# Two chunks of three units by feature tile in the input phase, the third chunk later, and head 1 behind group 0

## The chip, the cores and the metric

The kernel runs on one core of one Trainium2 chip. The metric is device time in microseconds (us) of one execution. A core has a matrix engine (PE, whose weight loads are shown as PEld), three engines for elementwise work (DVE, ACT, POOL) and a queue engine (SP) that issues most transfers. Each engine runs its own list of instructions in the order in which the program wrote them, and waits on semaphores for the others.

## The reference, cut to what matters

One step of a two-layer decoder over 1032 tokens (1024 of a prompt and 8 single samples, T = 1032), with 1024 features and fp32 data. Each layer begins with a modulated norm and one input projection, whose output is cut into four retention heads (v, k, q, g) and four gating groups (vv, u):

```python
mod = jax.nn.silu(c) @ w_ada + b_ada
sh1, sc1, gt1, sh2, sc2, gt2 = jnp.split(mod, 6, axis=-1)
h = modulate(rmsnorm(x, g_mix), sh1, sc1)      # rmsnorm(x)*g * (1 + sc1) + sh1
p = h @ w_in
q, k, v, g, u, vv = jnp.split(p, [...])
...                                             # retention heads, gating groups
mix = jnp.concatenate([o_ret, o_gm], axis=-1) @ w_out
x = x + gt1[:, None, :] * mix
...                                             # norm, up projection, conv, down projection
```

## The kernel before

Features lie on the 128 partitions (8 feature tiles k), tokens on the free axis, cut into three chunks of 344 columns. A **unit** is 128 output features for all 1032 tokens. Each fp32 product is made of three passes of fp32r products, hi*Hh, hi*Hl and lo*Hh, where `hi` and `lo` are the two parts of the weights (`split`: ACT copies hi, DVE subtracts for lo) and `Hh` and `Hl` those of the scaled input. A unit is thus 8 x 3 x 3 = 72 matmuls (L274 in `block`, L261 to L263 in `mm3`). The row factor of the norm (1/rms of each token) is not in Hh: it is multiplied in when the unit leaves PSUM (`rows_out`, L609, by the tile `R`).

PSUM holds two `big` buffers of three banks and two `side` buffers of one bank. The `tp` pool has 23 slots, which weights (`raw`, `hi`, `lo`), modulation weights (`ada`) and activations share.

**Start of layer 0.** All eight tiles of the scale part of `w_ada` are loaded and multiplied (`Ada.part`, L569), then transposed (L578), and only then are Hh (L419) and Hl (L420) made, chunk by chunk. `joint` computes the first two units (v and k of head 0) chunk by chunk. The sums of squares, `rsqrt` and their spread over the partitions (`inv_rms`, `spread`, L393) run beside it, and the shift part of `w_ada` (t0) between chunks 1 and 2. Both units are evacuated at the end. The units q and g of head 0 follow with `unit`.

**Side work.** What follows an evacuation (rotary product, transposes, retention state, group norm) are generators in the list `Side`. `tick` runs at most two steps of them after each feature tile of a unit; `drain` runs them with no unit work between until given tasks are done. The remaining parts of `w_ada` (`ada_t`, parts 2 to 5) are such tasks with the lowest priority.

**Order of units in layer 0, before:** head 0 (v, k, q, g), head 1, group 0, group 1, then the first output projection `partial`, whose three summands are head 0, head 1 and group 0 (`OUT_GROUPS[0] = (0, 1, 4)`). `mixes` drains the last task of these three first. The task chain of a head ends with `task_q` (retention, `row_norm`) and `task_o` (two halves of transposes, product with g, `split`). Nothing else orders the engines.

Of the kernel before, what the change touches and what calls it, by code (L numbers as in the profile page):

```python
# [43 lines left out]
BUDGET = 2  # L44
ADA = (1, 0, 2, 3, 4, 5)
KB = 1.31


class Task:
# [41 lines left out]
def tile_hybrid_decoder_step(  # L91
# [56 lines left out]
    for l in range(DEPTH):  # L148
# [240 lines left out]
    def spread(w, js=range(4)):  # L389

        r = sps()
        for j in js:
            nc.tensor.matmul(  # L393
                r[:, j * QW:(j + 1) * QW], ident[:, 32 * j:32 * j + 1].to_broadcast([128, 128]), w,
                start=True, stop=True)
        return r

    def to_dram(w):
        rd = dp.tile([4, QW], F32, tag="rd", name=f"rd{count[0]}")
        nc.gpsimd.dma_start(out=rd, in_=w[0:128:32])  # L400
        return rd
# [21 lines left out]
    def norm(c, hold, R, A, B, gate=None, dma=True):  # L423
# [6 lines left out]
        if dma:  # L430
            rd = to_dram(w)
        if c == 2 or not dma:
            r = spread(w, (3,) if dma else range(4))
        yield 1
        o = R[:, c * CW:c * CW + n]
        if dma:
            from_dram(o, rd)
        else:
            nc.scalar.activation(out=o, in_=r[:, 0:n], func=ACTF.Copy)
        if c == 2:  # L440
            q = small([128, KT, NB], "gs")
            ss = slice(SEQ, T)
            rb = r[:, CW - NB:CW].unsqueeze(1).to_broadcast([128, KT, NB])
            nc.vector.tensor_tensor(out=q, in0=XS, in1=rb, op=ALU.mult)
            nc.vector.tensor_tensor(out=q, in0=q, in1=A[:, :, 1:9], op=ALU.mult)
            nc.vector.tensor_tensor(out=q, in0=q, in1=B[:, :, 1:9], op=ALU.add)
            nc.scalar.activation(out=Hh[:, :, ss], in_=q, func=ACTF.Copy)
            nc.vector.tensor_tensor(out=Hl[:, :, ss], in0=q, in1=Hhf[:, :, ss], op=ALU.subtract)

    def norm_out(c, hold, xg, g, out, gate=None):  # L450

# [152 lines left out]

    def rows_out(ps, R, name):

        a, b = slot(name), small([128, 1], "wb", 4)
# [328 lines left out]
    with tc.manual_schedule():  # L936
# [9 lines left out]
        nc.vector.memset(ones_m, RS / D)  # L946
        nc.scalar.activation(out=scond, in_=craw, func=ACTF.Silu)

        def load_x(c, ms=slice(0, KT)):
            s = slice(c * CW, (c + 1) * CW)  # L950
            nc.sync.dma_start(out=X[:, ms, s], in_=xT[:, ms, s])

        A, B = mods[0][1], mods[0][0]
        adas[0].issue(8)
        W.issue(1)
        for ms in GROUPS3:
            load_x(0, slice(ms[0], ms[-1] + 1))
        W.issue(2)
        load_x(1)
        load_x(2)  # L960
        adas[0].issue(16)
# [5 lines left out]
        for c in range(NC3):  # L967
            for ms in GROUPS3:
                late = []
                scaled(c, ms, A, late)  # L970
                for f in late:
                    f()
                if c == 0 and ms[0] == 0:
                    W.prepare()
            for ms in GROUPS3:
                squares(c, ms, holds[c])
        next(ns[2])
        next(ns[0])
        t0 = adas[0].part(0, 8)

        def steps(*gs):
            for g, n in gs:
                for _ in range(n):
                    next(g, None)

        def start(c, i):
            if (c, i) == (1, 1):
                steps((t0, 2))
            if (c, i) == (2, 0):
                steps((ns[2], 1), (t0, 4), (ns[2], 1), (t0, 1), (ns[2], 1))  # L990
                columns(B)
                steps((ns[0], 1), (ns[1], 1))
            if (c, i) == (2, 1):
                steps((ns[0], 2), (ns[1], 1))
            if c == NC3:
                steps((ns[1], 2))

        for l in range(DEPTH):
            mod = mods[l]
# [181 lines left out]
```

## Time and profile before

| | us |
|---|---|
| median of three runs | 2087.15 (2087.12 to 2088.16) |
| profiled execution, whole | 2088.26 |
| its span in the trace | 2086.1 |
| PE busy | 2030.7 (97%) |
| DVE, ACT, POOL busy | 1173.6, 663.0, 69.6 |
| first product of a unit starts | 19.12 |
| head 0 (four units) multiplied | 95.34 |
| first product of the first `partial` | 230.32 |

All times are counted from the start of the span. A row of the trace's list of instructions gives the start, the busy time, engine, line, operation, output and inputs, how many instructions it merges, and in brackets how long the engine had been idle before and what ended that. A busy time includes a modelled tail of the matmul, so the spacing of two starts is the better price of one.

### The profile page before, as it was taken

Reading aid. Unit: us, or ns where it says so; the run is one execution under the profiler, and the core shown is the slowest. Engines: PE = TensorE matmul, PEld = TensorE weight load, DVE = VectorE, ACT = ScalarE, POOL = GpSimd, SP = SyncE. Lnnn points to the kernel's source line nnn. Section 1 sums busy time; section 2 is a strip of 40 time slices with the busy share of each in tenths; the row PEclk is TensorE's granted clock in tenths of the full one; section 3 lists DMA queues with packets and bytes.
Section 4 is the critical chain, followed back from the end, with each engine's and each line's share of the span. In section 5 each row is a group of like instructions: output and inputs, shape, how many; then the busy total and the mean of one; then the engine's idle time right before and its main releaser. Section 6 shows DMA issues by size and latency. Waiting matters only on the chain.

```text
span 2086.1 us, 32232 instructions
## 1 busy us (share of the span) xinstructions
PE 2030.7 (97%) x13806; PEld 1970.5 (94%) x13806; DVE 1173.6 (56%) x2087; ACT 663.0 (32%) x903; POOL 69.6 (3%) x155
## 2 busy tenths in 40 slices
PE   7999999999999999999999999999999999999997
PEld 5898999998898999999989999999999999999997
DVE  5356635676544456454673675457846545645566
ACT  4332223224422222324343331332433332241432
POOL 0000000000000000000000000000000000000001
PEclk9999999999999999999999999999999999999998
DMA  9344112112454211111121211121121011111012
GB/s 376 129 145 161 61 51 63 52 59 82 164 195 165 93 51 51 33 59 31 54 68 65 73 56 37 63 73 52 42 58 62 31 51 51 51 41 51 31 34 83
DMA packets 51886, 164.31 MB, mean 79 GB/s; under 512 B 6864, under 2 KB 14384, under 8 KB 51744
## 3 DMA queue, kind: packets, MB, share of 16 engines
q1 hardware_dynamic: 47616, 151.22, 21.6%
q0 software_dynamic: 3728, 10.50, 1.5%
q8 instruction: 109, 1.79, 0.3%
q10 hardware_dynamic: 400, 0.53, 0.1%
q14 instruction: 33, 0.27, 0.0%
HBM read 152.88 MB, written 9.61 MB: 78 GB/s over the span
## 4 chain that ended last, share of the span: by engine, by line
PE 86%; DVE 7%; ACT 3%; DMA 2%; issue 1%; SPq 0%; POOL 0%; POOLq 0%; DVEq 0%; ACTq 0%
PE big L274 74%; PE side L569 2%; DMA ada<-in_w_ada 2%; PE big L261 1%; PE big L262 1%; PE big L263 1%; PE side L618 1%; DVE lo L220 1%; DVE X L516 1%; ACT Hh L419 1%; ACT sq L351 1%; DVE Hl L420 1%; PE side L759 1%; PE side L730 1%; PE side L781 1%
## 5 line engine op out<-in xcount | busy, mean ns | idle before, releaser
L274 PE MATMUL big<-Hh,hi 128*128 128x344 f32 (+1 forms) x2496 | 546.8, 327 | 1.9 <-DVE v L609 1.9
L274 PE MATMUL big<-Hh,lo 128*128 128x344 f32 (+1 forms) x2496 | 533.5, 322 | 7.9 <-DVE lo L220 7.9
L274 PE MATMUL big<-Hl,hi 128*128 128x344 f32 (+1 forms) x2496 | 532.3, 321 | 0.0
L274 PEld LDWEIGHTS big<-Hh,lo 128*128 128x128 f32 x2496 | 423.1, 190 | 9.0 <-DVE lo L220 9.0
L274 PEld LDWEIGHTS big<-Hh,hi 128*128 128x128 f32 x2496 | 415.4, 190 | 17.0 <-issue 14.4
L274 PEld LDWEIGHTS big<-Hl,hi 128*128 128x128 f32 x2496 | 422.6, 189 | 0.0
L609 DVE TENSOR_TENSOR a<-big,R 128x1032 f32<-128x1032 f32 x64 | 78.9, 1233 | 270.6 <-ACT wb L608 270.6
L220 DVE TENSOR_TENSOR lo<-raw,hi 128x1024 fp32r<-128x1024 f32 x160 | 195.0, 1219 | 58.6 <-ACT hi L211 58.6
L899 DVE SCALAR_TENSOR_TENSOR c<-a,pars,c 128x1032 f32<-128x1032 f32 x128 | 165.0, 1290 | 111.4 <-ACT acol L892 77.7
L319 DVE SCALAR_TENSOR_TENSOR X<-big,mod,X 128x1032 f32<-128x1032 f32 x128 | 165.3, 1292 | 108.7 <-PE big L274 108.7
L608 ACT ACTIVATE wb<-big 128x1 f32<-128x1 f32 x112 | 18.9, 169 | 628.8 <-PE big L274 585.4
L211 ACT ACTIVATE hi<-raw 128x1024 fp32r<-128x1024 f32 x160 | 166.7, 1047 | 20.2 <-PE big L274 16.5
L274 PE MATMUL big<-ahi,hi 128*128 128x344 f32 x624 | 132.7, 321 | 0.0
L274 PE MATMUL big<-ahi,lo 128*128 128x344 f32 x624 | 131.8, 319 | 0.0
L274 PE MATMUL big<-alo,hi 128*128 128x344 f32 x624 | 131.7, 319 | 0.0
L274 PEld LDWEIGHTS big<-ahi,hi 128*128 128x128 f32 x624 | 104.2, 188 | 2.9 <-issue 1.6
L274 PEld LDWEIGHTS big<-alo,hi 128*128 128x128 f32 x624 | 104.6, 188 | 0.0
L274 PEld LDWEIGHTS big<-ahi,lo 128*128 128x128 f32 x624 | 104.3, 188 | 0.0
L889 ACT ACTIVATE a<-a,wb 128x1032 f32<-128x1032 f32 x64 | 74.1, 1158 | 83.5 <-DVE a L609 83.5
L925 ACT ACTIVATE ahi<-c 128x1032 fp32r<-128x1032 f32 x32 | 34.2, 1068 | 194.3 <-DVE c L923 192.5
L890 ACT ACTIVATE c<-a,pars 128x1032 f32<-128x1032 f32 x64 | 80.1, 1251 | 3.3
L261 PE MATMUL big<-Hh,hi 128*128 128x344 f32 (+1 forms) x192 | 64.3, 335 | 7.7 <-DVE X L516 5.0
(199 smaller groups left out, 2363.9 us busy)
## 6 DMA issues: line engine op xcount, KB each, us to landing
ada<-in_w_ada SPq DMA_DIRECT2D x96, 512.0 KB, 4.8
raw<-in_w_up SPq DMA_DIRECT2D x64, 512.0 KB, 3.5
raw<-in_w_in SPq DMA_DIRECT2D x48, 512.0 KB, 3.6
raw<-in_w_down SPq DMA_DIRECT2D x32, 512.0 KB, 3.5
raw<-in_w_out SPq DMA_DIRECT2D x16, 512.0 KB, 3.5
S<-in_s_ret POOLq DMA_DIRECT2D x8, 512.0 KB, 4.1
vb<-vd SPq DMA_DIRECT2D x8, 512.0 KB, 4.6
out_rs<-S POOLq DMA_DIRECT2D x8, 512.0 KB, 4.6
```

What stands on the lines that cost most here:

```text
L211: nc.scalar.activation(out=hi[:, 0:1024], in_=self.raw[i][:, 0:1024], func=ACTF.Copy)
L220: nc.vector.tensor_tensor(out=lo[:, 0:1024], in0=self.raw.pop(i)[:, 0:1024], in1=self.split[i][0].bitcast(F32)[:, 0:1024], op=ALU.subtract)
L261: nc.tensor.matmul(out, whi, rhi, start=start, stop=False)
L262: nc.tensor.matmul(out, whi, rlo, start=False, stop=False)
L274: nc.tensor.matmul(ps[:, c, 0:n], w, r[:, s], start=st, stop=sp_)
L319: nc.vector.scalar_tensor_tensor(out=v3(X[:, m]), in0=ps[:, :, 0:CW], scalar=gt[:, m, 0:1], in1=v3(X[:, m]), op0=ALU.mult, op1=ALU.add)
L569: nc.tensor.matmul(ps[32 * j:32 * j + 32, 0:256], scond[:, k, :], w[:, j * 256:(j + 1) * 256], start=(k == 0), stop=(k == KT - 1), tile_po ...
L609: nc.vector.tensor_tensor(out=v3(a), in0=ps[:, :, 0:CW], in1=v3(R), op=ALU.mult)
L889: nc.scalar.activation(out=a[:, 0:T], in_=a[:, 0:T], func=ACTF.Identity, bias=b)
L890: nc.scalar.activation(out=c[:, 0:T], in_=a[:, 0:T], func=ACTF.Identity, scale=w[2], bias=col(l, P_CB + i))
L899: nc.vector.scalar_tensor_tensor(out=c[:, off:off + T], in0=a[:, 0:T], scalar=wt, in1=c[:, off:off + T], op0=ALU.mult, op1=ALU.add)
L925: nc.scalar.activation(out=hi[:, 0:T], in_=c2[:, 0:T], func=ACTF.Copy)
```

## The change

It touches only layer 0 up to the first `partial`.

- The scale part is no longer summed over all features first. `scale_weights(j)` loads for feature tiles 2j, 2j+1 only (two transfers of 512 KB, rows of 1 KB), `scale_sums` multiplies, `scale_out` adds the four partial sums and transposes with the 0/1 matrix `sel`. X is loaded by feature tile (rows of 4128 B), and `operand(m)` makes Hh and Hl of one tile for all 1024 prompt tokens.
- `warm(n)` issues n matmuls of 512 columns on a constant tile `wm`, which nothing reads: 9, 2 and 7 of them before the first real product.
- The first three units (v, k, q) run with the feature tile as the outer loop, over two chunks, in six banks of the two `big` buffers.
- All rows' squares are summed at once (`row_sums`), one `rsqrt` over 258 columns, three `spread`s, and R is ready for the two chunks' evacuation (`first_chunks`).
- `fourth` then runs the remaining shift products, two chunks of unit g, and the third chunk of all four units, and evacuates v, k, q and g one after another.
- In layer 0 group 0 now comes ahead of head 1, in the list of weight pieces and in the order of units: head 0, group 0, head 1, group 1, `partial`.
- `shift = adas[0].part(0, 2)` is the same generator as before, on an `Ada` object on which nothing was issued by then; its `issue` counts tiles from 0.

```diff
-        for p in h0[2:] + head(1) + group(0) + group(1):
+        for p in h0[2:] + (head(1) + group(0) if l else group(0) + head(1)) + group(1):
...
-        adas[0].issue(8)
...
-        side.drain(side.add(adas[0].part(1, 8, 1)))
-        W.prepare()
         R = rows_scale()
-        holds = [[], [], []]
-        ns = [norm(c, holds[c], R, A, B, dma=False) for c in range(NC3)]
...
+        wm = slot("wm", F32R)
+        nc.vector.tensor_copy(wm[:, 0:512], ones_m[:, 0:1].to_broadcast([128, 512]))
+        warm(9)
+        shift = adas[0].part(0, 2)
+        sw = {0: scale_weights(0)}
+        W.issue(1)
+        load_x(0)
...
+        t = scale_sums(sw[0])
+        warm(2)
+        scale_out(0, t)
+        warm(7)
+        W.high()
+        operand(0)
+        W.low()
+        operand(1)
...
+        for j in range(4):
+            order = [(2 * j + kk, i) for kk in range(2) for i in range(3)]
+            if j == 3:
+                order.sort(key=lambda q: q[1])
+            for n, (k, i) in enumerate(order):
+                hi, lo = W.tile(u, i * 8 + k)
+                passes(hi, lo, k, [(place[i][c][0][:, place[i][c][1], 0:CW], c * CW, CW) for c in range(2)])
...
+                if j < 3 and n == SUMS[j]:
+                    t = scale_sums(sw[j + 1])
+                if j < 3 and n == SUMS[j] + 2:
+                    scale_out(j + 1, t)
+                    operand(2 * j + 2)
+                    operand(2 * j + 3)
...
+                if j == 1 and n == 5:
+                    next(shift)
...
+                if j == 3 and n == 0:
+                    w = row_sums()
+                if j == 3 and n == 2:
+                    next(shift)
+                if j == 3 and n == 3:
+                    rows(w, rs8)
+                    first_chunks(0)
+                if j == 3 and n == 5:
+                    first_chunks(1)
+        first_chunks(2)
+
+        def fourth(evac):
+            for _ in range(3):
+                next(shift)
...
+            ps = big()
+            for k in range(KT):
+                hi, lo = W.tile(u4, k)
+                passes(hi, lo, k, [(ps[:, c, 0:CW], c * CW, CW) for c in range(2)])
...
+            rest = big()
+            for i in range(4):
+                out = (rest[:, i] if i < 3 else ps[:, 2])[:, 0:CW + 2]
+                for k in range(KT):
+                    hi, lo = W.tile(u, i * 8 + k) if i < 3 else W.tile(u4, k)
+                    passes(hi, lo, k, [(out, 2 * CW, CW + 2)])
...
-                joint(ev[:2], (), range(NC3), start)
+                fourth(ev)
...
-            run_units(ev[2:])
-            run_units(heads[1].evacs())
-            run_units(grps[0].evacs())
+            run_units(ev[4 if l == 0 else 2:])
+            for o in (heads[1], grps[0]) if l else (grps[0], heads[1]):
+                run_units(o.evacs())
             run_units(grps[1].evacs())
```

**PE at the start of the program, before.** `ada` and `scond` are the modulation's factors, `big` is a unit's accumulator:

```order
L569 MATMUL side_144<-ada_115,scond 32x256 x4
L569 MATMUL side_144<-ada_117,scond 32x256 x4
L578 MATMUL side_179<-ident,adat_177 128x128 x2
L261 MATMUL big_282<-Hh,hi_184 128x344
L262 MATMUL big_282<-Hl,hi_184 128x344
L263 MATMUL big_282<-Hh,lo_188 128x344
```

**PE at the start of the program, now:**

```order
L1014 MATMUL side_107<-wm_105 128x512 x9
L972 MATMUL side_145<-ada_117,scond 32x256 x4
L972 MATMUL side_145<-ada_119,scond 32x256 x4
L1014 MATMUL side_156<-wm_105 128x512 x2
L982 MATMUL side_159<-sel_103,adat_154 128x16 x2
L1014 MATMUL side_164<-wm_105 128x512 x7
L1008 MATMUL big_192<-Hh,hi_172 128x344 x2
L1008 MATMUL big_192<-Hl,hi_172 128x344 x2
L1008 MATMUL big_192<-Hh,lo_176 128x344 x2
```

Two groups of modulation products stand ahead of the first product where eight stood, and 18 constant products stand around them.

**PE at the end of group 1's unit u and the start of the first `partial`, before.** `big_1939` is the unit, `big_2143` the first output tile of `partial`; `hi_1502` and `hi_1993` are weights and a head's mix:

```order
L274 MATMUL big_1939<-Hl,hi_1835 128x344 x2
L274 MATMUL big_1939<-Hl,hi_1835 128x346
L274 MATMUL big_1939<-Hh,lo_1898 128x344 x2
L274 MATMUL big_1939<-Hh,lo_1898 128x346
L274 MATMUL big_2143<-hi_1502,hi_1993 128x344 x3
L274 MATMUL big_2143<-lo_1503,hi_1993 128x344 x3
```

**The same place of PE now.** L568 is a modulation step, L846 and L863 are group 1's transposes and gating products, L619 and L804 the transposes of head 1's output `o` and `os`:

```order
L568 MATMUL side_2025<-ada_2081,scond 32x256 x4
L568 MATMUL side_2025<-ada_2083,scond 32x256 x4
L846 MATMUL side_2114<-ident,os_1898 128x128
L863 MATMUL side_2120<-wst_518,vn_1826 128x128 x4
L568 MATMUL side_2025<-ada_2102,scond 32x256 x4
L568 MATMUL side_2025<-ada_2104,scond 32x256 x4
L619 MATMUL side_2136<-ident,o_1987 128x128 x4
L863 MATMUL side_2142<-wst_518,vn_1826 128x128 x4
L619 MATMUL side_2149<-ident,o_1987 128x128 x4
L804 MATMUL side_2155<-ident,os_1924 128x128
L275 MATMUL big_2165<-hi_1568,hi_1863 128x344 x3
L275 MATMUL big_2165<-lo_1569,hi_1863 128x344 x3
```

Between the unit and `partial` stands side work with no unit's products among it.

**DVE at that place, before.** `u_2120` is the unit's evacuation, `X<-big_2143` takes the first output of `partial`, L632 and L634 belong to group 1's norm:

```order
L188 TENSOR_TENSOR lo_2052<-mix_1923,hi_2051 128x1032
L220 TENSOR_TENSOR lo_2091<-raw_1837,hi_2046 128x1024
L629 BN_STATS st_2097<-vn_1956 128x6 x8
L629 BN_STATS st_2097<-os_2072 128x6
L609 TENSOR_TENSOR u_2120<-big_1939,R_190 128x1032
L632 BN_AGGR mv_2098<-st_2097 128x2 x9
```

**DVE at that place now**, from the last step of head 1's norm (`o_1987`) to the second part of its mix (`lo_2162`):

```order
L645 TENSOR_SCALAR o_1987<-o_1987,mv_2039,fac_2040 128x128 x8
L645 TENSOR_SCALAR os_1924<-os_1924,mv_2039,fac_2040 128x128
L849 TENSOR_SCALAR vrows<-side_2114,pars 128x8
L850 TENSOR_SCALAR ss_2116<-vrows,pars 128x8
L865 SCALAR_TENSOR_TENSOR mix_2119<-side_2120,pars,bsb_519 128x512
L869 TENSOR_TENSOR mix_2119<-mix_2119,u_2010 128x512
L800 SCALAR_TENSOR_TENSOR mix_2127<-side_2136,pars,g_1690 128x512
L865 SCALAR_TENSOR_TENSOR mix_2119<-side_2142,pars,bsb_519 128x512
L869 TENSOR_TENSOR mix_2119<-mix_2119,u_2010 128x512
L800 SCALAR_TENSOR_TENSOR mix_2127<-side_2149,pars,g_1690 128x512
L806 SCALAR_TENSOR_TENSOR mix_2127<-side_2155,pars,g_1690 128x2 x4
L189 TENSOR_TENSOR lo_2162<-mix_2127,hi_2161 128x1032
```

Before, head 1's mix was split on DVE ahead of the last unit's evacuation; now its norm and split come behind it.

## Rows read from the trace of the kernel before

**Rows 1.** Busy time by stretch: length, then PE, PEld, DVE, ACT, POOL; clock, DMA share, GB/s.

```profile
0.00:19.12 19.12, 9.33 (x66) 1.92 (x66) 1.22 (x4) 3.66 (x6) 4.54 (x12) 1.00 0.92 333
19.12:59.34 40.22, 37.15 (x306) 33.38 (x306) 27.55 (x69) 22.39 (x40) 0.64 (x1) 1.00 0.95 365
...
95.34:230.32 134.98, 131.25 (x1010) 119.89 (x1009) 74.31 (x198) 39.60 (x56) 5.24 (x7) 1.00 0.41 139
230.32:2086.10 1855.78, 1821.36 (x12211) 1787.27 (x12209) 1059.75 (x1808) 585.30 (x786) 56.22 (x132) 1.00 0.20 65
```

**Rows 2.** List of instructions, PE at the start, and the last slow products.

```profile
13.15 2.29 PE L569 MATMUL side<-ada,scond 128*32 128x256 f32 x16 [0.19 <-DMA ada<-in_w_ada]
...
17.23 0.69 PE L578 MATMUL side<-ident,adat 128*128 128x128 f32 x2 [0.50 <-ACT adat L574]
...
29.34 0.49 PE L262 MATMUL big<-Hl,hi 128*128 128x344 f32 x1
...
29.62 0.45 PE L263 MATMUL big<-Hh,lo 128*128 128x344 f32 x1
...
29.91 0.33 PE L261 MATMUL big<-Hh,hi 128*128 128x344 f32 x1
```

**Rows 3.** The same list, PE where `joint` ends and the next units begin.

```profile
58.33 1.02 PE L393 MATMUL side<-rw,ident 128*128 128x86 f32 x8
61.29 0.75 PE L274 MATMUL big<-Hh,hi 128*128 128x344 f32 x3 [1.95 <-DVE v L609]
...
64.94 1.23 PE L274 MATMUL big<-Hh,lo 128*128 128x344 f32 x3 [2.42 <-DVE lo L220]
...
71.10 1.07 PE L569 MATMUL side<-ada,scond 128*32 128x256 f32 x16
```

**Rows 4.** The same list, DVE: a weight's lo, a 1032-column product, an rsqrt step.

```profile
18.37 1.22 DVE L220 TENSOR_TENSOR lo<-raw,hi 128x1024 fp32r<-128x1024 f32 x1
...
434.00 1.28 DVE L319 SCALAR_TENSOR_TENSOR X<-big,mod,X 128x1032 f32<-128x1032 f32 x1
...
50.08 0.25 DVE L341 SCALAR_TENSOR_TENSOR rw<-rw 128x86 f32<-128x86 f32 x1
```

**Rows 5.** Transfers, first 60 us: GB/s in 40 slices of 1.5 us; issue to landing.

```profile
GB/s 0 150 306 418 399 394 297 393 407 426 393 372 387 399 371 377 369 377 372 414 418 401 421 399 429 407 423 403 407 397 423 385 415 415 412 145 262 257 183 22
...
ident<-in_ident POOLq DMA_DIRECT2D x1, 64.0 KB, 3.9
```

**Rows 6.** The chain of waits by merged pieces: a long run of unit products.

```profile
249.57 32.70 PE big L274 x207
```

**Rows 7.** List of instructions, an evacuation and a head's norm near the second `partial`.

```profile
402.17 1.23 DVE L609 TENSOR_TENSOR u<-big,R 128x1032 f32<-128x1032 f32 x1 [6.18 <-ACT wb L608]
...
403.44 1.16 ACT L823 ACTIVATE u<-u,wb 128x1032 f32<-128x1032 f32 x1 [1.30 <-DVE u L609]
...
405.06 0.70 DVE L632 BATCH_NORM_AGGREGATE mv<-st 128x2 f32<-128x6 f32 x9
...
407.90 2.13 DVE L644 TENSOR_SCALAR vn<-vn,mv,fac 128x128 f32<-128x128 f32 x8
...
410.21 2.14 DVE L644 TENSOR_SCALAR o<-o,mv,fac 128x128 f32<-128x128 f32 x8
```

**Rows 8.** The same list, head 1's last steps before the first `partial`.

```profile
217.50 1.16 PE L862 MATMUL side<-wst,vn 128*128 128x128 f32 x8 [0.84 <-DVE mix L799]
...
218.69 0.75 DVE L864 SCALAR_TENSOR_TENSOR mix<-side,pars,bsb 128x512 f32<-128x512 f32 x1 [1.25 <-PE side L862]
...
219.48 0.69 DVE L868 TENSOR_TENSOR mix<-mix,u 128x512 f32<-128x512 f32 x1
...
220.23 0.60 DVE L805 SCALAR_TENSOR_TENSOR mix<-side,pars,g 128x2 f32<-128x2 f32 x4
...
220.87 1.06 ACT L187 ACTIVATE hi<-mix 128x1032 fp32r<-128x1032 f32 x1 [7.83 <-DVE mix L805]
...
221.96 1.23 DVE L188 TENSOR_TENSOR lo<-mix,hi 128x1032 fp32r<-128x1032 f32 x1 [1.13 <-ACT hi L187]
```

More of the change, by code (lines that the diff above doesn't have):

```diff
@@ L46 @@
 KB = 1.31
+SUMS = (2, 1, 1)
 class Task:
@@ L429, in norm @@
         yield 5
[L430 to L433, printed above, removed]
+        rd = to_dram(w)
+        if c == 2:
+            r = spread(w, (3,))
         yield 1
[L435 to L439, printed above, removed]
-        if c == 2:
[L441 to L448, printed above, removed]
+        from_dram(R[:, c * CW:c * CW + n], rd)
+        if c == 2:
+            samples(r[:, CW - NB:CW], A, B)
     def norm_out(c, hold, xg, g, out, gate=None):
@@ L605, in rows_out @@
     def rows_out(ps, R, name):
+        if isinstance(ps, tuple):
+            return ps
         a, b = slot(name), small([128, 1], "wb", 4)
@@ L955, in tile_hybrid_decoder_step, with warm @@
+        def warm(n):
+            ps = sps()
+            for _ in range(n):
+                nc.tensor.matmul(ps, wm[:, 0:128], wm[:, 0:512], start=True, stop=True)
+        wm = slot("wm", F32R)
[3 more added lines that the diff above has]
+        sw = {0: scale_weights(0)}
         W.issue(1)
-        for ms in GROUPS3:
-            load_x(0, slice(ms[0], ms[-1] + 1))
-        W.issue(2)
+        load_x(0)
@@ L959, in tile_hybrid_decoder_step @@
         load_x(1)
-        load_x(2)
-        adas[0].issue(16)
-        side.drain(side.add(adas[0].part(1, 8, 1)))
-        W.prepare()
-        R = rows_scale()
-        holds = [[], [], []]
-        ns = [norm(c, holds[c], R, A, B, dma=False) for c in range(NC3)]
[L967 to L996, printed above, removed]
+        W.issue(3)
@@ new lines, in tile_hybrid_decoder_step @@
+        for j in (1, 2):
+            sw[j] = scale_weights(j)
+            load_x(2 * j)
+            load_x(2 * j + 1)
+        load_x(6)
+        load_x(7)
+        R = rows_scale()
+        t = scale_sums(sw[0])
[6 more added lines that the diff above has]
+        operand(1)
+        W.high()
+        W.low()
+        W.high()
+        W.low()
+        u = list(W.get()) + list(W.get())
+        banks = [big(), big()]
+        place = [[(banks[(2 * i + c) // 3], (2 * i + c) % 3) for c in range(2)] for i in range(3)]
@@ new lines, in tile_hybrid_decoder_step, with row_sums @@
+        sums = []
+        def row_sums():
+            q = small([128, KT, NB], "gs")
+            nc.scalar.activation(out=q, in_=XS, func=ACTF.Square)
+            for a, ms in zip(sums, GROUPS3):
+                nc.vector.tensor_reduce(
+                    out=a[:, SEQ:T], in_=q[:, ms[0]:ms[-1] + 1].rearrange("p m b -> p b m"), axis=AX.X, op=ALU.add)
+            ps = sps()
+            for i, a in enumerate(sums):
+                av = a[:, 0:T].rearrange("p (c q n) -> p q c n", c=NC3, q=4)
+                for j in range(4):
+                    nc.tensor.matmul(
+                        ps[32 * j:32 * j + 32, 0:NC3 * QW].rearrange("p (c n) -> p c n", c=NC3), ones_m, av[:, j],
+                        start=(i == 0), stop=(i == 2), tile_position=(0, 32 * j))
+            w = slot("rw")[:, 0:3 * NC3 * QW].rearrange("p (s n) -> p s n", s=3)
+            nc.vector.tensor_scalar(
+                out=w[:, 0], in0=ps[:, 0:NC3 * QW], scalar1=EPS * RS, scalar2=None, op0=ALU.add)
+            rsqrt(w[:, 0], w[:, 1], w[:, 2])
+            return w[:, 1]
@@ new lines, in rows, with square @@
+        def rows(w, rs8):
+            for c in range(NC3):
+                n = CW if c < 2 else CW - NB
+                r = spread(w[:, c * QW:(c + 1) * QW])
+                nc.scalar.activation(out=R[:, c * CW:c * CW + n], in_=r[:, 0:n], func=ACTF.Copy)
+                if c == 2:
+                    nc.scalar.activation(out=rs8, in_=r[:, n:CW], func=ACTF.Copy)
+        def square(m):
+            t = slot("sq")
+            nc.scalar.activation(out=t[:, 0:SEQ], in_=X[:, m, 0:SEQ], func=ACTF.Square)
+            if m in (0, 3, 6):
+                sums.append(t)
+            else:
+                a = sums[-1]
+                nc.vector.tensor_tensor(out=a[:, 0:SEQ], in0=a[:, 0:SEQ], in1=t[:, 0:SEQ], op=ALU.add)
```

101 lines of the change are left out of this document (97 added, 4 removed).

## Prediction

> **What bounds the kernel now.** I read the stretches first, then the list of instructions at the two places that the change rewrites. PE is busy for 131.25 of 134.98 us between the end of head 0's products and the first `partial`, and for 1821 of 1856 us after it [rows 1]. A unit's matmul costs 32.70/207 = 0.158 us there [rows 6], so in both stretches the sum of matmuls is the time, and only PE's gaps can be won or lost. Head 0 is different: its 288 matmuls are 288 x 0.158 = 45.5 us, and they end at 95.34. Three losses are visible. The first product starts at 19.12, behind eight modulation tiles [rows 1, 2]. PE then runs slowly until about 29.9: two starts are 0.28 us apart [rows 2] against 0.158, which is the lower of the two clock levels (1.2 against 2.4 GHz), although the clock column says 1.00. After `joint` PE waits 1.95 us for v's evacuation and 2.42 us for the next weights, and the products that start at 64.94 are slow again (1.23 us for three); by 71.10 a modulation step of 16 records takes 1.07 us instead of 2.29 [rows 2, 3].
>
> The span is 2086.1 us in the profiled execution and the median is 2087.15, so I add 1.05 us to a span.
>
> **Part 1, up to the first dense product (S).** The constant products need `wm`, whose cast stands behind the reduction of `ident` on DVE, and `ident` needs 3.9 us to land after an early POOL issue [rows 5]: about 5.5, and 6.3 with the two DVE steps. Nine products of 512 columns at the slow price (512/344 x 0.285 = 0.43 us) end at 10.2. The two modulation groups behind them cost 2.29 [rows 2]: 12.5. Copying the sums takes about 0.5, the selector 0.5 (between the slow 0.69 of the transposes [rows 2] and half of it), the two small DVE steps 0.5, Hh of tile 0 on ACT 1.05 (as a copy of 1032 columns [rows 8]): 15.1. Then DVE is the engine that PE waits for: Hl, lo, Hl, lo, lo stand in this order, at 1.15 to 1.25 us each [rows 4]: 21.1. With the last products of tile 0, **S = 21.4**. I take the clock as fast by then: before, the products from 19.12 ran slow and those after 29.9 fast [rows 2], and here products begin at 6.3. If the clock is slow at S, because PE waits between 15 and 21, the next products run at half speed, as those from 64.94 to 71 did [rows 3], which costs 2.5 to 3 us more. Ends: S = 19.8 (fast from 10) to 24.
>
> **Part 2, from S to the fourth unit (F).** PE has 126 matmuls (19.9), three sums of modulation (3 x 1.07), three selectors (0.8), row sums (12 matmuls of 258 columns, about as long as 1.5 modulation groups of 256: 1.6), three spreads at 1.0 each [rows 3] and four shift steps at 1.07: 32.8 us. Waits: each new pair of feature tiles needs selector, DVE, ACT and DVE again (0.5 + 1.05 + 1.25), of which 6 or 12 matmuls (1.0 or 1.9 us) hide a part, so PE waits about 1.7, 0.7 and 0.8 us; the row sums wait for the last Hl and its reductions (0.7); nine rsqrt steps over 258 columns (0.25 for 86 [rows 4], so about 0.43 each, 3.9 us) lie under 18 matmuls and a shift step (3.9 us) with 0.3 us left. That is 4.2, and F = 21.4 + 37 = 58.4.
>
> Transfers set a second bound. `shift` counts tiles from 0, so its first `issue` loads eight scale tiles that nothing reads (4.2 MB), ahead of the ten that are used. Up to the last shift tile 21.5 MB are to be moved; at the 400 GB/s of the slices from 4.5 to 52.5 us [rows 5] that ends near 56.5, and its product at 57.6. The two bounds fall together, and I keep F = 58.4. Rows of 1376 B (X, the slices from 16.5 to 28.5) move at about 375 GB/s against some 410 of the 4 KB rows [rows 5]; the new 1 KB rows (4.2 MB) may lose as much and the longer X rows win it back.
>
> The Trainium skill (DMA: Bandwidth & Descriptors, Specifications) gives about 358 GB/s as a core's limit from HBM. By it the fourth unit would start near 64 and the sum below would be 5 to 6 us higher; the slices of the trace stay near 400 for 45 us, so I give that 0.03.
>
> **Part 3, end of head 0.** 48 matmuls and the transposes of the shift are 7.9 us; 96 matmuls of 346 columns and v's transposes 16.1. Head 0 is multiplied at 58.4 + 24.0 = **82.4** instead of 95.34: 12.9 us earlier. The first part of the change works.
>
> **Part 4, what comes behind.** Against the 131.25 us of PE work from there to `partial` [rows 1], 4.0 us are added, because part 2 of `w_ada` (four steps at 1.0), which before ran inside head 0's units, now runs behind; and 1.9 us move from behind the start of `partial` to ahead of it (group 1's transposes and gating products, now drained). The first unit of group 0 needs the `big` buffer of g, which is evacuated last: 2.1 us of waiting, like the 1.95 of v [rows 3]. ACT reloads its function tables twice more; nothing waits for ACT there.
>
> **The drain** is the largest term. Head 1 is now followed by two units instead of four. Its chain does not fit under them: in the new order of PE all of it, from the last output product of head 1 on, stands between group 1's last product and `partial`, with no unit's products among it, and the rest of part 5 of `w_ada`. From the last product (t = 0): evacuation of u starts at 0.4, ACT is done with it at 2.8 [rows 7], copies the second half of o (0.6), DVE takes its statistics (1.0): 4.5. From the aggregation to the end of the scaling of vn and o are 7.3 us [rows 7]: 11.8, and two small steps, 12.4. From here the transposes and gating products go one behind another, since one `side` buffer is held by the modulation sums; the trace shows that wait (0.84 us on DVE's mix) [rows 8]. A gating product with its DVE step takes 217.50 to 219.44, 1.94 us, a half of o's transposes about 1.4 beside the second gating step of 0.69 [rows 8]: 14.3, 15.7, 17.7, 19.1. From the last small DVE products to lo are 220.23 to 223.19, 3.0 us: **22.4**. Queued behind this on PE is the whole `partial`: nine products on head 0's mix can go at 19.4, the rest waits for hi and lo. Useful PE work within the 22.4 us: output products 1.75, four modulation steps at most 4.0, the transposes and gating products 2.4, and 12 products of `partial` 1.9, together 10.1. So PE idles 12.3 us, 7 of them in one piece. Gaps of 1.95 and 2.42 us close together were enough to lose the fast clock before [rows 3]; I add 2.6 us for about 5.5 us of products at half speed, as from 64.94 to 71. Before, this place cost 134.98 - 131.25 = 3.7 us with all gaps of the stretch; 0.9 of them lie earlier and stay.
>
> **Sum.** 82.4 + 131.25 + 4.0 + 1.9 + (2.1 + 0.9 + 12.3 + 2.6) = 237.5 for the start of `partial` at full rate, and 1855.8 - 1.9 behind it: 2091.4, against 2086.1. The time is 2091.4 + 1.05 = **2092**, 0.25% slower. In short: 12.9 us won, 4.0 only moved, 14 lost again in the gaps.
>
> **The rivals.**
> - *The gain is kept (faster).* If the drain costs little, the start's 12.9 less 4.0 and 2.1 remain: 2080 to 2082. It decides at a drain of under 5 us in all (gap and clock). For it: DVE is busy only 74 of 135 us there [rows 1], so steps could start earlier than I chain them. Against it: PE's order is fixed, and head 1's norm alone takes 12 us of DVE and ACT after the last product. 0.11.
> - *The start is lost too (slower).* The clock is slow at S, or the shift tiles land late because SP waits for slots ahead of them. From the point where F lies beyond 62, the time is 2096 to 2100. For it: from 15 to 21 PE waits for DVE between pairs of products. Against it: S moves little, and a gap of 1.95 us followed by products left them fast at 61.29 [rows 3]. 0.14, with the transfer limit above.
> - *A wash.* S and F at their early ends and a short slow spell after the drain: 2087 to 2089, no change to be measured. 0.17.
> - The forecast's case, 2089 to 2096: 0.58.
>
> **How the numbers follow.** A measurement of this kernel can tell about 0.2%, 4.2 us, from no change: the limits are 2083 and 2091.3. The forecast's case lies for six parts in ten above the upper one: 0.36 slower, 0.22 the same. With the rivals, slower 0.50, same 0.39, faster 0.11. The range 2083 to 2099 leaves out most of the first rival and the end of the second.
>
> **What would show it.** Right: the ninth constant product ends near 10, the dense products begin near 21 with 0.158 us spacing, head 0 ends at 80 to 85, and ahead of the first `partial` PE has about 12 us of idle time behind DVE, followed by some 5 us of products 0.28 us apart. Wrong: PE idle for under 6 us there; slow products between 21 and 30; a wait of over 3 us for shift tiles ahead of the fourth unit; or new waits after `partial`, which I take as unchanged.

## The result, and the profile after

The changed kernel takes **2112.35 us** (2111.4 to 2113.97) against 2087.35 (the kernel before, with a fourth run beside the three of its table): a ratio of 1.012 (95% interval 1.0102 to 1.0137), 25 us slower, and beyond the end of the predicted range. The profiled span is 2109.6 us, 18.2 above the sum of 2091.4.

The stretches of core 0 come first; the columns are the stretch, its length, the busy time of each engine with its count of records, PE's granted clock, DMA share and GB/s:

```profile
core 0: us, PE busy (x) PEld busy (x) DVE busy (x) ACT busy (x) POOL busy (x), PEclk, DMA share, GB/s
0.00:21.78 21.78, 13.43 (x56) 9.15 (x57) 8.16 (x11) 9.01 (x10) 4.53 (x12) 0.90 0.95 327
21.78:24.40 2.62, 2.62 (x20) 1.35 (x20) 0.00 (x0) 0.39 (x1) 0.00 (x0) 0.51 1.07 396
24.40:61.98 37.58, 33.80 (x281) 26.98 (x280) 20.84 (x33) 15.45 (x20) 0.00 (x0) 1.00 0.95 374
61.98:88.82 26.84, 24.66 (x160) 24.02 (x156) 4.22 (x11) 10.82 (x17) 1.74 (x3) 1.00 0.22 76
88.82:227.73 138.91, 130.66 (x986) 117.68 (x985) 71.52 (x174) 40.73 (x57) 7.16 (x8) 0.99 0.40 138
227.73:257.00 29.27, 21.57 (x130) 13.80 (x130) 18.23 (x63) 5.36 (x8) 0.00 (x0) 0.65 0.49 176
257.00:2109.60 1852.60, 1817.35 (x12171) 1783.18 (x12169) 1048.33 (x1772) 581.80 (x781) 56.46 (x132) 1.00 0.20 65
```

The marks are: the last product of feature tile 0 ends at 21.78 (the prediction's S), the clock rises at 24.40, the fourth unit starts at 61.98 (F), head 0 is multiplied at 88.82, group 1's last product of a unit ends at 227.73, and `partial` runs at full rate by 257. Before, head 0 ended at 95.34 and `partial` began at 230.32 [rows 1].

PE's own list at the start (start, busy time, engine, line, operation, tiles, records; the wait ahead in brackets) answers to [rows 2]:

```profile
6.28 4.21 PE L1014 MATMUL side<-wm 128*128 128x512 f32 x9 [6.28 <-DVE wm L1017]
10.41 1.19 PE L972 MATMUL side<-ada,scond 128*32 128x256 f32 x16
...
14.40 0.58 PE L1008 MATMUL big<-Hh,hi 128*128 128x344 f32 x2
...
19.19 0.94 PE L1008 MATMUL big<-Hh,lo 128*128 128x344 f32 x2 [0.79 <-DVE lo L221]
...
21.78 1.93 PE L972 MATMUL side<-ada,scond 128*32 128x256 f32 x16
...
24.38 0.49 PE L1008 MATMUL big<-Hl,hi 128*128 128x344 f32 x2
```

Sixteen modulation records take 1.19 us at 10.41, behind the constant products, and 1.93 at 21.78: the clock had risen and fallen again while PE waited between tile 0's products.

The rest of head 0 has these rows, the sums and spreads of the squares and then the third chunks; they answer to [rows 3]:

```profile
46.88 1.95 PE L1060 MATMUL side<-sq,ones_m 128*32 128x258 f32 x24
...
54.61 1.12 PE L394 MATMUL side<-rw,ident 128*128 128x86 f32 x8 [0.55 <-ACT R L1073]
...
74.73 0.42 PE L1008 MATMUL big<-Hh,hi 128*128 128x346 f32 x1 [0.88 <-DVE v L1163]
...
80.55 0.43 PE L1008 MATMUL big<-Hh,hi 128*128 128x346 f32 x1 [1.30 <-DVE k L1163]
```

Between 88.82 and 227.73 PE idles 8.25 us, in seven waits. Three of them, with the DVE rows ahead of the last:

```profile
108.53 0.66 PE L619 MATMUL side<-ident,vv 128*128 128x128 f32 x4 [0.78 <-ACT kt L718]
112.84 0.66 PE L619 MATMUL side<-ident,vv 128*128 128x128 f32 x4 [1.35 <-DVE S L738]
...
179.96 1.23 DVE L189 TENSOR_TENSOR lo<-mix,hi 128x1032 fp32r<-128x1032 f32 x1 [3.33 <-ACT hi L188]
...
183.52 1.23 DVE L665 TENSOR_TENSOR k<-k,ks 128x1032 f32<-128x1032 f32 x1
184.67 0.23 DVE L580 TENSOR_TENSOR mod<-side,pars 128x72 f32<-128x72 f32 x1
184.89 1.09 PE L619 MATMUL side<-ident,k 128*128 128x128 f32 x4 [3.00 <-DVE mod L580]
```

A step of one chain (vv's or k's transposes) stands in PE's order, the row puts its wait down to a step of another chain on ACT or DVE, and the unit's products wait behind it. (For the wait of 3.00 us the step that the row names isn't the one, see e8.) The other four waits are 0.84, 0.52, 0.69 and 1.08 us, the last for a tile of `w_ada` at 207.34. The drain ahead of `partial` is the place of [rows 8]:

```profile
232.11 0.68 PE L568 MATMUL side<-ada,scond 128*32 128x256 f32 x8 [2.43 <-ACT u L824]
...
235.63 1.08 PE L568 MATMUL side<-ada,scond 128*32 128x256 f32 x8 [1.24 <-DMA ada<-in_w_ada]
...
243.33 1.94 PE L568 MATMUL side<-ada,scond 128*32 128x256 f32 x16
...
247.16 1.16 PE L863 MATMUL side<-wst,vn 128*128 128x128 f32 x8 [0.84 <-DVE mix L800]
249.16 0.71 PE L619 MATMUL side<-ident,o 128*128 128x128 f32 x4 [0.84 <-DVE mix L865]
...
250.84 1.21 PE L275 MATMUL big<-hi,hi 128*128 128x344 f32 x3
...
253.01 1.23 DVE L189 TENSOR_TENSOR lo<-mix,hi 128x1032 fp32r<-128x1032 f32 x1 [1.18 <-ACT hi L188]
...
256.18 0.77 PE L275 MATMUL big<-hi,hi 128*128 128x344 f32 x3
```

From the last product of a unit to the first of `partial` are 23.1 us, and the products up to 256.18 start 0.86 us apart for three, nearly twice the 0.47 that follow. At full rate the work between 227.73 and 257.00 is 12.7 us (output products 1.8, sums 4.3, transposes 1.1, gating products 1.8, 23 products of `partial` 3.7), so the place loses 29.3 - 12.7 = 16.6 us: 7.7 of PE standing idle (29.27 less 21.57 busy) and 8.9 of the lower clock.

### The profile page after: what moved, and what is told of

It reads as the page before. It is cut to its first block, busy times and chain, and to the rows that moved or that the text cites. A ratio compares the mean times of both kernels' runs of the same rounds, so it can differ in the third digit from the quotient of the medians.

```text
span 2109.6 us, 32207 instructions
## 1 busy us (share of the span) xinstructions
PE 2044.1 (97%) x13790; PEld 1976.2 (94%) x13790; DVE 1171.3 (56%) x2064; ACT 663.6 (31%) x892; POOL 69.9 (3%) x155
## 4 chain that ended last, share of the span: by engine, by line
PE 86%; DVE 8%; ACT 3%; DMA 1%; issue 1%; POOL 0%; POOLq 0%; DVEq 0%; ACTq 0%
PE big L275 72%; PE side L568 2%; PE big L1008 2%; PE side L619 1%; PE big L263 1%; PE big L262 1%; PE big L264 1%; DVE lo L221 1%; DVE X L515 1%; ACT Hh L420 1%; DMA ada<-in_w_ada 1%; ACT sq L352 1%; DVE Hl L421 1%; PE side L731 1%; PE side L782 1%
## 5 line engine op out<-in xcount | busy, mean ns | idle before, releaser
L275 PE MATMUL big<-Hh,hi 128*128 128x344 f32 x2448 | 535.8, 327 | 0.0
L275 PE MATMUL big<-Hh,lo 128*128 128x344 f32 x2448 | 522.0, 321 | 5.5 <-DVE lo L221 5.5
L275 PE MATMUL big<-Hl,hi 128*128 128x344 f32 x2448 | 521.6, 321 | 0.0
L275 PEld LDWEIGHTS big<-Hh,hi 128*128 128x128 f32 x2448 | 407.1, 190 | 13.8 <-issue 13.1
L275 PEld LDWEIGHTS big<-Hh,lo 128*128 128x128 f32 x2448 | 413.9, 189 | 6.4 <-DVE lo L221 6.4
L275 PEld LDWEIGHTS big<-Hl,hi 128*128 128x128 f32 x2448 | 414.2, 189 | 0.0
L609 ACT ACTIVATE wb<-big 128x1 f32<-128x1 f32 x109 | 18.4, 169 | 638.5 <-PE big L275 595.1
L212 ACT ACTIVATE hi<-raw 128x1024 fp32r<-128x1024 f32 x160 | 166.5, 1046 | 20.8 <-PE big L275 16.6
L515 DVE SCALAR_TENSOR_TENSOR X<-big,mod,X 128x344 f32<-128x344 f32 (+1 forms) x96 | 49.0, 565 | 19.3 <-PE big L264 19.2
```

The source lines that it names most:

```text
L212: nc.scalar.activation(out=hi[:, 0:1024], in_=self.raw[i][:, 0:1024], func=ACTF.Copy)
L275: nc.tensor.matmul(ps[:, c, 0:n], w, r[:, s], start=st, stop=sp_)
L515: nc.vector.scalar_tensor_tensor(out=xs, in0=ps[:, j, 0:n], scalar=gt[:, m, 0:1], in1=xs, op0=ALU.mult, op1=ALU.add)
```

## The experiments

**What does the order of the units cost?** Two kernels: the change with the old order, and the old input phase with the new order. The first also starts the modulation sums later, because they had no free slots at head 0's end.

```diff
 # e1: the changed kernel (the list of weight pieces likewise)
-            for o in (heads[1], grps[0]) if l else (grps[0], heads[1]):
-                run_units(o.evacs())
+            run_units(heads[1].evacs())
+            if l == 0:
+                for p in range(2, 6):
+                    ada_t[p] = side.add(adas[0].part(p, 2), ...)
+            run_units(grps[0].evacs())
 # e2: the kernel before (pieces likewise)
-            run_units(heads[1].evacs())
-            run_units(grps[0].evacs())
+            for o in (heads[1], grps[0]) if l else (grps[0], heads[1]):
+                run_units(o.evacs())
```

> The changed kernel with head 1 again ahead of group 0 in layer 0; the modulation steps of w_ada parts 2 to 5 start behind head 1 (with all the slots taken at head 0's end they can't start earlier in this order). Theory A (the order of the units gives the gain back, by the drain ahead of the first partial and the waits of its side work): 2085 to 2090, with PE idle for under 5 us in the 25 us ahead of the first partial. Rival B (the new input phase does it: head 0's four evacuations come close together and its backlog of small steps is what blocks later units, whatever the order): 2104 to 2112, with the waits of 0.5 to 3 us inside the units still there.

> The kernel before, with its old input phase, and only group 0 moved ahead of head 1 in layer 0 (units and weights). Theory A: the drain of head 1 costs here too, 12 us of idle and some 3 us of slow clock: 2100 to 2107. Rival B (the order costs nothing by itself): 2085 to 2090.

Measured: e1 2089.76 us, ratio 1.0012 (1.0003 to 1.0022); e2 2108.75 us, 1.0098 (1.0083 to 1.0113). e1 lies in theory A's range, e2 1.75 us beyond its end and far from rival B: in the kernel before, the order alone costs 21 us. The stretches of e2, from head 0's end to group 1's last product and on to `partial`, and PE's rows there:

```profile
95.34:233.90 138.56, 132.39 (x1001) 120.36 (x999) 67.32 (x171) 41.39 (x57) 5.24 (x7) 0.99 0.40 134
233.90:251.03 17.13, 6.00 (x31) 4.45 (x29) 14.00 (x59) 2.02 (x4) 0.00 (x0) 0.70 0.07 27
```

```profile
245.08 2.08 PE L862 MATMUL side<-wst,vn 128*128 128x128 f32 x8 [4.94 <-DVE mod L581]
```

`partial` begins at 251.03, 20.7 us later than the 230.32 of before. Over both stretches PE idles 17.3 us against 3.7 [rows 1], and the clock is low for part of the rest: eight gating products take 2.08 us at 245.08, and 1.16 at full clock [rows 8]. In e1 the largest wait of the last 25 us ahead of `partial` is 0.52 us.

**How long is the cover that is missing?** e6 puts one unit of group 0 behind head 1: the order is vv of group 0, head 1, u of group 0, group 1.

```diff
-            for o in (heads[1], grps[0]) if l else (grps[0], heads[1]):
-                run_units(o.evacs())
+            n0 = 0 if l else 1
+            run_units(grps[0].evacs()[:n0])
+            run_units(heads[1].evacs())
+            run_units(grps[0].evacs()[n0:])
```

> The changed kernel with the order vv of group 0, head 1, u of group 0, group 1: three units behind head 1 instead of two. Theory A (head 1's chain of small steps is longer than the two units of 11.4 us that follow it): the third unit covers 11 of the 23 us from the last product to partial, 2093 to 2099. Rival B (what costs is the collision of head 1's steps with group 0's, or any departure from the old order): 2105 to 2112.

Measured: 2095.65 us, ratio 1.0038 (1.0025 to 1.0052): 16.7 less than with two units. From the last product of a unit (222.6) to `partial` are 7.7 us here, against 23.1: one more unit covers most of the chain. What is left is its end, with the lower clock behind it:

```profile
227.25 0.66 PE L619 MATMUL side<-ident,o 128*128 128x128 f32 x4 [2.55 <-DVE mix L800]
230.21 0.48 PE L804 MATMUL side<-ident,os 128*128 128x128 f32 x1 [2.31 <-DVE mix L800]
230.34 1.21 PE L275 MATMUL big<-hi,hi 128*128 128x344 f32 x3
```

**Idle time or clock?** e5 keeps PE at work in the drain.

```diff
+                fill = big()
+                while not all(t.done for t in wait):   # last tasks of heads 0, 1 and group 0
+                    side.tick(0.5)
+                    nc.tensor.matmul(fill[:, 0], Hh[:, 0, 0:128], Hh[:, 0, 0:512], start=True, stop=True)
```

> The changed kernel with one constant product of 512 columns behind each step of side work from the end of group 1's products to the first partial. Theory A (a good part of what this place costs is PE at the lower clock from 233 to 256 us, where 8 modulation products take 1.08 us instead of 0.64 and the first partial's products 0.86 per three): 4 to 7 us are won, 2105 to 2108, with 0.158 us per product of partial from its first. Rival B (the idle time alone counts, and the filling stands in the way of the chain): 2110 to 2116.

Measured: 2109.14 us, ratio 1.0103 (1.0089 to 1.0117), 3.2 below the changed kernel and between the two expectations. PE's rows of e5:

```profile
236.63 1.07 PE L568 MATMUL side<-ada,scond 128*32 128x256 f32 x16
...
249.87 0.63 PE L275 MATMUL big<-hi,hi 128*128 128x344 f32 x3
```

The sums and the first products of `partial` are at full clock (1.07 us for 16, 0.47 us between starts), yet `partial` begins at 249.87 instead of 250.84, 22.5 us behind the last product of a unit (227.37) against 23.1: it isn't the lower clock that makes the chain long. The clock is worth about 3 us here (the intervals of the two ratios overlap, but each of e5's four times lies below all four of the changed kernel); the rest of the place is waiting.

**Do the modulation sums hold the chain up?** e8 starts parts 3 to 5 behind the first `partial`.

```diff
-                for p in range(2, 6):
+                for p in (2,):
                     ada_t[p] = side.add(adas[0].part(p, 2), ...)
 ...
             partial(mixes(OUT_GROUPS[0]), gt1, True)
+            if l == 0:
+                for p in range(3, 6):
+                    ada_t[p] = side.add(adas[0].part(p, 2), ...)
```

> The changed kernel with the modulation steps of parts 3 to 5 starting behind the first partial; part 2 stays where it is. Theory A (the steps of head 1 are held up by the modulation sums, which keep one of two side buffers for four steps and wait for their tiles, as the waits of 3.0, 1.08, 1.24 and 0.52 us say): 2098 to 2106. Rival B (head 1's own chain of DVE and ACT sets the drain and the sums only stand beside it): 2109 to 2114.

Measured: 2106.02 us, ratio 1.0089 (1.0073 to 1.0104), at the edge of A. The sums cost 6 us here, but not by the mechanism that I read from the wait of 3.00 us. Rows of PE, and one of DVE, in e8:

```profile
171.32 1.23 DVE L189 TENSOR_TENSOR lo<-mix,hi 128x1032 fp32r<-128x1032 f32 x1 [3.32 <-ACT hi L188]
...
176.25 0.63 PE L619 MATMUL side<-ident,k 128*128 128x128 f32 x4 [3.21 <-DVE k L665]
...
219.76 0.45 PE L846 MATMUL side<-ident,os 128*128 128x128 f32 x1 [4.92 <-DVE mv L633]
...
225.09 1.11 PE L619 MATMUL side<-ident,o 128*128 128x128 f32 x4 [3.17 <-DVE vrows L849]
```

The wait ahead of k's transposes is still there without the sums, now put down to k's rotary product. In the changed kernel that product (183.52 + 1.23 = 184.75) ended 0.15 us ahead of the modulation row that got the blame. In both kernels DVE had stood idle 3.3 us (179.96 and 171.32) for the copy `hi` of head 0's mix, which stands on ACT behind three steps of q's evacuation, and k's three rotary products stand behind that split in DVE's order. In e1 the wait ahead of the same transposes is 0.25 us (134.67).

What the sums do cost lies in the drain. From the last product of a unit (212.9) to `partial` (229.07) are 16.2 us here, against 23.1. Up to the last wait for the norm (225.09) it is 12.2 us against 13.6 (241.33); what follows takes 4.0 us instead of 9.5, with a gating product already done and no sum of `w_ada` in between.

**Is the new input phase faster by itself?** e7 is the kernel before with the sums started behind head 1, as in e1.

```diff
+            run_units(ev[2:])
+            run_units(heads[1].evacs())
             if l == 0:
                 for p in range(2, 6):
                     ada_t[p] = side.add(adas[0].part(p, 2), ...)
-            run_units(ev[2:])
-            run_units(heads[1].evacs())
```

> The kernel before with the modulation steps of w_ada parts 2 to 5 starting behind head 1, as in e1_order_back. Theory A (these steps are the same PE work wherever they stand, so all of e1's difference to this kernel is the new input phase): 2086 to 2089. Rival B (their late start costs by itself, by fewer units to hide in): 2090 to 2094, and the input phase alone would then be worth 2 us or more.

Measured: 2092.67 us, ratio 1.0023 (1.0013 to 1.0034): rival B. Starting the sums late costs 5 us by itself, and e1, with the same late start, is 2 to 3 us faster than e7, though the intervals of the two ratios overlap. The start of g's evacuation, the end of head 0, says the same; first e1, then e7:

```profile
88.57 1.23 DVE L610 TENSOR_TENSOR g<-big,R 128x1032 f32<-128x1032 f32 x1 [3.59 <-ACT wb L609]
```

```profile
90.63 1.23 DVE L609 TENSOR_TENSOR g<-big,R 128x1032 f32<-128x1032 f32 x1 [0.94 <-ACT wb L608]
```

With part 2 taken out of it, the old input phase ends 2.1 us behind e1's, and 1.1 us behind that of the changed kernel (89.53), where the sum counted 8.9 (12.9 less 4.0).

**The unread tiles and the constant products.** e3 leaves out the eight tiles, e4 the 18 products, and e11 both of them in e1.

```diff
+        adas[0].i = 8                       # e3, e11
         shift = adas[0].part(0, 2)
-        warm(9)                             # e4, e11, like warm(2) and warm(7)
```

> The changed kernel without the eight w_ada tiles (4.2 MB) that nothing reads. If the chain of PE, DVE and ACT sets the start of the fourth unit (61.98 us), as its row shows no wait for a DMA: within 2 us of the changed kernel, 2110 to 2114. Rival (transfers set it, and the w_ada queue stays late until the drain): 2102 to 2107, with the first dense product unchanged at 21.8 and the fourth unit at 57 to 59.

> The changed kernel without the 18 constant products. If they bring the clock up in time: the products behind the first dense one run at half speed for longer, and the time is 3 to 5 us above the changed kernel, 2115 to 2118. Rival (the clock has fallen again by 21.8 us, as the spacing of 0.28 us until 24.4 suggests, so they buy nothing): within 1 us, 2111 to 2113.5.

> e1_order_back without the 18 constant products and without the eight unread w_ada tiles; the order of all other instructions is that of e1. Theory A (neither does anything for the time, as e3 and e4 say: the transfers are not the bound, and the clock has fallen again by 21.8 us with the products there): within 1.5 us of e1, 2088 to 2091. Rival B (in e1 the input phase is the only thing left that differs, so its transfers and its clock show): without the tiles 2 us or more faster, 2085 to 2087.5, or without the products 2 us or more slower, 2091.5 to 2094.

Measured: e3 2111.45 (ratio 1.0115, 1.01 to 1.013), e4 2111.29 (the same ratio and interval), e11 2089.83 (1.0011, 1.0002 to 1.002). None of them changes the time by as much as can be measured, but the reason is not that they do nothing. PE's rows of e4:

```profile
15.45 0.77 PE L1008 MATMUL big<-Hh,hi 128*128 128x344 f32 x2
16.03 0.78 PE L1008 MATMUL big<-Hl,hi 128*128 128x344 f32 x2
...
19.09 1.07 PE L972 MATMUL side<-ada,scond 128*32 128x256 f32 x16
...
40.95 0.62 PE L982 MATMUL side<-sel,adat 128*128 128x16 f32 x4 [2.14 <-ACT adat L976]
```

Without the products S is 19.09, 2.7 us **earlier**: the first product of a unit starts at 12.26 instead of 14.40. The products of tile 0 run at the lower clock (0.58 us for two), but from 18.35 on at full clock. Then PE waits 2.14 us for a copy on ACT that stands behind squares of X, whose rows wait for transfers (2.25 us ahead of the first), and the clock falls twice more, to 0.67 from 40.9 to 46 us and to 0.62 from 55 to 59.5, which is some 3.4 us. So the fourth unit starts at 62.25, no earlier than the 61.98 of the changed kernel. With the unread tiles in place the transfers are a bound on F close to PE's: the wait for that copy is 1.40 us in e1. e3, with a late S (21.47), starts the fourth unit at 61.72; e11, which leaves out both, at 60.29, the earliest of these, with no wait for ACT at 40 us. There the clock then falls between the spreads (0.50 from 54 to 56 us), and g's evacuation starts at 87.89 against 88.57 in e1.

**Can the old order have the early sums?** e9 is the changed kernel with the old order and the sums where the change has them, each tile loaded one step ahead instead of two. e10 also puts the third chunk of k in a side buffer and leaves the unread tiles out.

```diff
-                    ada_t[p] = side.add(adas[0].part(p, 2), ...)
+                    ada_t[p] = side.add(adas[0].part(p, 0), ...)       # e9, e10
-                out = (rest[:, i] if i < 3 else ps[:, 2])[:, 0:CW + 2]
+                out = (sps() if i == 1 else rest[:, i] if i < 3 else ps[:, 2])[:, 0:CW + 2]   # e10
-                    if i:
+                    if i > 1:                                          # e10
                         side.tick(KB / 3)
```

> The changed kernel with head 1 again ahead of group 0 in layer 0, and the modulation steps of w_ada parts 2 to 5 starting behind head 0 as in the changed kernel, their tiles loaded one step ahead instead of two. Theory A (the new input phase ends head 0 about 1.5 to 2 us earlier than the old one once part 2 is taken out of both; the late start of the sums is what cost e7 its 5 us): 2084 to 2086. Rival B (the later products wait for tiles that are loaded a step later, or for head 0's four evacuations that come close together): 2088 to 2094.

> As e9_back_early_sums, with the third chunk of the second unit (k) in a side buffer instead of the second bank of the big buffer that the first unit's third chunk is evacuated from, and without the eight unread w_ada tiles. Theory A (the two waits of 0.88 and 1.30 us on the evacuations of v and k come from the shared buffer): head 0 ends 2 us earlier than in e9, and the time is 1.5 to 2.5 us below e9's. Rival B (the steps that then find one side buffer only, v's transposes, move the same wait behind): within 0.7 us of e9.

Measured: e9 2098.37 (ratio 1.0046, 1.0032 to 1.006), e10 2107.69 (1.0094, 1.008 to 1.0107). Both expectations failed: e9 is 12 us above theory A and 4 above rival B, and e10 is 9 us slower than e9, where both theories had it as fast or faster. Rows of PE in e9, then in e10:

```profile
110.42 0.66 PE L619 MATMUL side<-ident,v 128*128 128x128 f32 x4 [1.35 <-DVE S L738]
117.82 0.27 PE L696 MATMUL side<-ident,v 128*8 128x128 f32 x1 [1.34 <-DVE S L738]
139.75 0.67 PE L769 MATMUL side<-S,qm 128*32 128x128 f32 x16 [1.29 <-issue]
```

```profile
155.82 1.08 PE L568 MATMUL side<-ada,scond 128*32 128x256 f32 x8 [3.64 <-DMA ada<-in_w_ada]
...
242.17 0.87 PE L568 MATMUL side<-ada,scond 128*32 128x256 f32 x8 [1.76 <-DMA ada<-in_w_ada]
```

In e10 the two waits on v and k are gone and g's evacuation starts at 87.34 instead of 88.55, but between 88 us and `partial` PE waits much more (20.1 us in all waits, about 8 of them for tiles loaded one step ahead). e9 waits 10.8 us there (144.85 less 134.03 busy), against 4.0 in e1 (127.85 less 123.88). Which share comes from the shorter load distance and which from the head's chains was not separated.

**The best that was found.** e12 is e1 without the unread tiles, with part 2 behind head 1 and parts 3 to 5 behind `partial`.

> e1_order_back without the unread tiles, with w_ada part 2 starting behind head 1 and parts 3 to 5 only behind the first partial. Theory A (the sums collide with the steps of the heads wherever both stand close together, and behind the first partial they lie under longer products): 2085 to 2088, with PE idle for under 3 us from 88 us to the first partial. Rival B (the same sums then collide with the side work of heads 2 and 3): 2089 to 2095, with the first partial 9 us earlier than in e1 and all of it given back by the second.

Measured: 2088.61 us, ratio 1.0003 (0.9994 to 1.0012), between the expectations: as fast as the kernel before, and no faster. From 88.5 to 219 us PE idles 3.4 us, but the sums meet the steps of heads 2 and 3 later, with waits of 0.69 us at 331 and 335 us, so the earlier `partial` (212.15, against 214.55 in e1) isn't kept. No kernel here beats the one before.

## Why the prediction was wrong

The direction and the cause of the drain were right, and its size near; two other terms were each about 7 us too small. From the predicted span to the measured one, by the steps of the prediction:

- **S**: 21.78 against 21.4, near, but in part by luck: the sum took the clock as fast by then, and it is 0.51 from 21.78 to 24.40. At full clock, in e1, S is 20.13. This differs between executions (below); with the products S lies between 19.9 and 21.9.
- **F**: 61.98 against 58.4. The waits were right (3.8 us idle, 4.2 predicted), the work was not: 36.4 us busy against 32.8. Of the 3.6, the low clock behind S is 1.3, row sums (1.95 against 1.6) and spreads (1.1 against 1.0 each) 0.7; the other 1.6 are spread over some 300 records. The step was too short whatever the clock did: e1, at full clock, has S at 20.13 and F at 61.01, and there PE waits 1.40 us at 41.28 for the same copy as in e4. That the bounds of PE and of the transfers lie close together was right, only 3 us later.
- **End of head 0**: 88.82 against 82.4. The 24.0 of part 3 became 26.84; 2.2 of it are the two waits for a shared big buffer, which the sum had for the first unit behind head 0 and not for the third chunks. With F that is 6.4 us of the 12.9 won. Against a start with part 2 taken out, as in e7, the gain is 1 to 2 us where the sum counted 12.9 - 4.0 = 8.9: part 2 took about 5 us there (95.74 less 90.63), not 4.0.
- **The wait for g's big buffer**: 2.1 predicted, 0 measured. Group 0's first unit starts at 88.82.
- **Waits within the units** up to 227.73: 8.25 us idle and about 1.4 at the lower clock, against 0.9 (and the 2.1 above). This is the step that failed most, with the end of head 0. I took over the 0.9 us of the old order as if waits belonged to the units, and wrote that nothing waits for ACT there (part 4). Waits belong to how chains of side work meet: the largest, 3.00 us, comes from a split on DVE that waits 3.33 us for ACT, and the order of the units changes it (0.25 in e1). The order alone, in e2, makes 6.2 us of idle time in its units (138.56 less 132.39), where the kernel before has 3.7 in all. Whether the backlog of head 0 adds to it, as e9 may say, was not separated from the load distance.
- **The drain**: 16.6 us lost against 12.3 + 2.6 = 14.9. That the totals are near is in part luck. The chain of 22.4 us, up to the `lo` of head 1's mix, took 26.5 (253.01 + 1.23 less 227.73): the norm 13.6 against 12.4, the transposes and gating products 9.5 against 7.0, the last split 3.4 against 3.0. Against these 4.1 us, 0.8 more of useful work lay in the chain, and of the slow products of `partial` only 1.0 us of loss came behind it, where 2.6 was counted. PE idles 7.7 us instead of 12.3, in pieces of at most 2.43 and not 7, since the sums and gating products run at the lower clock in between; e5 wins 3.2 by a full clock. With 16.6 us lost the first rival, which needs under 5, was wrong, though DVE is busy only 18.2 of 29.3 us there.
- **Behind `partial`**: 2.4 us more than the 1853.9 counted. About 2 of it lie behind 560 us, at places that differ between runs of the same order (below); it was not pursued.

With 0.4 + 3.2 + 2.8 for head 0, 7.7 for the units (waits 6.7 more and about 1 of work), 1.7 for the drain and 2.4 behind, the 18.2 us are accounted for. The median lies another 1.7 above the predicted time: I added 1.05 to a span, and here the median is 2.75 above it, since before's profiled execution was 1.1 above its median and this one 0.2 below.

The transfer rival, by the Trainium skill's figure of 358 GB/s (DMA: Bandwidth & Descriptors, Specifications), doesn't hold here. Two stretches of the changed kernel show 405 and 411 GB/s:

```profile
28.00:40.00 12.00, 10.44 (x76) 8.68 (x80) 7.53 (x8) 8.18 (x10) 0.00 (x0) 1.00 1.04 405
40.00:52.00 12.00, 11.32 (x99) 8.51 (x92) 8.40 (x18) 3.84 (x6) 0.00 (x0) 1.00 1.03 411
```

The rival "the start is lost too", with its F of 62 just reached, named the right loss, but priced without the waits that follow: 2096 to 2100.

## What to carry to other kernels

A chain of small steps that a later stage needs must have as much other work of PE behind it as the chain is long: here two units behind head 1 left 23.1 us of its chain uncovered, three left 7.7, and the four of the old order left none. The third unit gave back 17 of 25 us. When units change places, the waits between chains of side work have to be counted anew for every unit, not carried over from the old trace. A gain at the start is the difference to a start without the work that is moved behind it, and that difference is best measured by moving that work alone (e7).

## What the runs showed of the hardware

The granted clock after the same gap differs between executions. In the input phase of the second layer the changed kernel and e4 run the same products with the same gap (1.86 us at 1562.94 and 1.85 at 1562.87, the only one in this stretch), and one is at 0.83 in it, the other at 1.00; first the changed kernel, then e4:

```profile
1560.00:1570.00 10.00, 8.14 (x42) 7.86 (x42) 6.00 (x5) 3.94 (x7) 0.00 (x0) 0.83 0.19 54
```

```profile
1560.00:1570.00 10.00, 8.14 (x52) 7.86 (x51) 6.00 (x5) 3.88 (x7) 0.00 (x0) 1.00 0.18 54
```

That is 1.7 us, for which the sum had no term. The input phase shows the same: over 12 to 24 us the granted clock is 0.72 to 0.74 in three traces of the kernels with the constant products (the changed one, e3, e6), 0.86 in two (e8, e10) and 1.00 in four (e1, e5, e9, e12), with no wait over 1.2 us between tile 0's products in any. So the products, behind which 16 modulation records take 1.07 to 1.54 us at about 10 us, didn't secure it.

In both kernels without the products (e4, e11) the column says 1.00 as well, but there it can't be taken at its word: the products of tile 0 start 0.29 us apart until about 18.4 us in e4 and 18.9 in e11, and 0.16 apart behind that. The kernel before shows the same, 0.28 apart at a column of 1.00 [rows 2]. At the start of a program the spacing of the rows is what tells the clock.
